# u, v and z as blocks with seven-product quads: a new order of the work, and x's place given to the branch inputs

## The chip, the cores and the metric

One core of a Trainium2 chip runs the whole kernel. The metric is the device time of one execution in microseconds (us). Matrix products run on TensorE (PE), elementwise work on VectorE (DVE) and ScalarE (ACT), a few small things on GpSimd (POOL); SyncE (SP) issues nearly all DMAs.

## The reference, cut to what matters

```
h = rms_norm(x, norm_g)                      # x: 256 x 4096 float32
proj = h @ w_in                              # 4096 x 22560
u, v, z_gm, qkv, z_dn, b, a, gate_gm, gate_dn = split_columns(proj)
y_gm = gmlp_spatial_gating(gelu(u), gelu(v), ln_g, ln_b, w_s, b_s)   # layer norm of v, 16 mixing matrices
y_gm = (y_gm * silu(z_gm)) @ w_br_gmlp       # 2048 x 4096
q, k, v = silu(causal_conv(qkv)) ...         # 16 heads of 128
o = rms_norm(gated_delta_rule(q, k, v, beta, g), dn_norm_g)
y_dn = (o * silu(z_dn)) @ w_br_dn            # 2048 x 4096
merged = sigmoid(gate_gm) * y_gm + sigmoid(gate_dn) * y_dn
out = rms_norm(x + merged @ w_out, final_g)  # 4096 x 4096
```

## The kernel before, in words

**Jobs.** `jobs` is a list of products with a weight matrix. A `Job` makes one chunk of 512 columns for both halves of the 256 rows: it walks over k in *pieces* of two k tiles of 128. Each float32 weight tile is loaded as `raw`, cast to a high part `wh` (ACT, L185) and a low part `wl` (DVE, L186); per k tile and row half three matmuls of 512 columns are issued (L196 to L198), so a piece has 12, a job over 4096 rows 192, a branch job (2048 rows) 96. x, as high and low part, lies in the eight `xs` tiles.

**Blocks.** A `Block` makes two neighbouring chunks together. For a pair of k tiles (a *quad*) the plain way needs 8 products of three matmuls; for the quads in `SEVEN` it needs 7, by a Strassen-Winograd scheme: pieces a, b, d, c (L225 to L230), with combinations of weights made on DVE (`tt`, L264 to L272) and combinations of x prepared once (`gforms`). Eight sums P1 to P8 fill all eight PSUM banks; `sums_out` (L987) adds them up into the two chunks. Only 12 of the 16 gate chunks are blocks here.

**Order.** Gates 0 and 2, six gate blocks, then for four groups of heads the jobs v, k, q, z of the delta part, then v0 to v3, gate 13, u0, z0, ... u3, z3, gate 15, 16 branch jobs (dn and gmlp of a chunk alternate), 8 jobs with `w_out`.

**Lanes.** Everything else is written as generators in two `lanes`: lane 0 takes what a finished job leaves (activations, convolutions, layer norm, mixing), lane 1 the delta rule of the groups (`dn_gen`, L765). `step` (L121) advances each lane to its next `yield`; `stream` (L282) calls it after every 12 matmuls. `drain` steps until a lane is empty. The order so written is a priority: the compiler's scheduler issues what is ready, so loads, ACT and DVE work may come earlier than written if nothing holds them.

**The delta part of a group.** `done_conv` scales a job's result, stores it, loads it back shifted three times and multiplies by `conv_w`; then `dn_gen` makes the 32x32 blocks (L776 to L816), inverts them by an elimination of 62 DVE operations (L825, L827), builds the 128x128 inverses by PE steps (L860 to L908), and makes o (L912 to L968), stored to `yds`. The branch inputs `ygs`, `yds` are loaded back as `yr` and cast to `ys` in `open_c` (L1027) during gate 15, into two `yr` buffers.

**Memory.** Pools are opened and closed in phases; a tile put where an older one was waits for that tile's last use. `px` (gate blocks), `pa` and `pq` (delta), `pv` and `pb` (gMLP), `pc` (branches), `pd` (output). `xs` is kept all along and takes the branch results at the end (L1078).

Of the kernel before, what the change touches and what calls it, by code (L numbers as in the profile page):

```python
# [9 lines left out]
F32 = mybir.dt.float32  # L10
# [23 lines left out]
SEVEN = (1, 3, 4, 6, 8, 9, 11, 13)  # L34

# [9 lines left out]
class Block:  # L45
# [3 lines left out]
    def __init__(self, w, col, nk, src, forms, done, before=None):  # L49
        self.w, self.col, self.nk, self.src, self.forms = w, col, nk, src, forms  # L50
        self.done, self.before = done, before
# [11 lines left out]
def trunk(ctx, tc, t):  # L63
# [4 lines left out]
    xtp = ctx.enter_context(tc.tile_pool(name="xtp", bufs=1))  # L68
# [49 lines left out]
    lanes = [[], []]  # L118
    wait = [0, 0]

    def step():  # L121
        for i, q in enumerate(lanes):
            if wait[i] > 0:
# [80 lines left out]
    def block_acc():  # L204

        nblk[0] += 1
        apart = ("P6", "P7") if nblk[0] % 2 == 0 else ("P3", "P8")
        return {n: bank() if n in apart else pm.tile([P, 512], F32, name="acc")
                for n in ("P8", "P4", "P2", "P3", "P1", "P6", "P5", "P7")}
# [51 lines left out]
    def quad_split(p, raw):  # L261
        r0, r1 = raw
        if p.kind == "a":
            t12 = px.tile([P, 2, NC], F32, name="tt", bufs=3)  # L264
            t34 = px.tile([P, 2, NC], F32, name="tt", bufs=3)
            V.tensor_tensor(out=t12[:, 0], in0=r0[:, 0], in1=r0[:, 1], op=ALU.add)
            V.tensor_tensor(out=t12[:, 1], in0=t12[:, 0], in1=r1[:, 0], op=ALU.subtract)
            h = px.tile([P, 1, NC], F32R, name="s2", bufs=7)
            l = px.tile([P, 1, NC], F32R, name="s2", bufs=7)
# [12 lines left out]
    def stream():  # L282
# [12 lines left out]
        state = dict(got=0, made=0, pairs=0, mm=0)  # L295

        def get(upto):
            while state["got"] < min(upto, len(order)):
# [3 lines left out]
                where = "wp" if room["wp"] else "x" if room["x"] and quad else None  # L302
# [8 lines left out]
                else:  # L311
                    raw = (wp if where == "wp" else px).tile([P, KPD, NC], F32, name="raw",
                                                             bufs=5 if where == "wp" else XRAW)
                    nc.sync.dma_start(out=raw, in_=j.w[k * P:(k + 1) * P, j.col:j.col + 2 * NC].rearrange(
                        "p (c n) -> p c n", c=2))
# [5 lines left out]
        def make():  # L321
            p = pieces[state["made"]]
            n = order.index(p.raws[-1])
            get(n + (4 if p.kind == "std" else 4 + XRAW))
# [13 lines left out]
        for c, p in enumerate(pieces):  # L338
# [4 lines left out]
            if p.first:  # L343
                if j.before:
                    j.before()
                acc = block_acc() if isinstance(j, Block) else [pm.tile([P, 512], F32, name="acc") for _ in range(2)]
            u = sp.pop(c)
            if isinstance(j, Block):
                quad_mms(p, *u, acc)
# [10 lines left out]
            state["mm"] += {"a": 3, "b": 6, "c": 6, "d": 6}.get(p.kind, 12)  # L360
            if state["mm"] >= 12:
                state["mm"] -= 12
                step()
# [6 lines left out]
    phx = ExitStack()  # L370
    px = phx.enter_context(tc.tile_pool(name="px", bufs=1))
    xraw = {}

    def first_x(i):
        if i < KT // KPD:
            xraw[i] = px.tile([P, KPD, S], F32, name="s2", bufs=7)
# [23 lines left out]
    def norm_gen():  # L400
        yield 12
        xend = xs[KT // 4 - 1][:, 1, 3, S - 1:S].bitcast(F32)
        for m in range(2):
            for c in range(8):
                xt = px.tile([P, NC], F32, name="s2", bufs=7)
# [32 lines left out]

    gforms = {q: px.tile([P, 2, 4, P], F32R, name=f"gf{q}") for q in SEVEN}

# [7 lines left out]
    def forms_gen():  # L448
        yield 15
        for q in SEVEN:  # L450
            x = xs[q // 2]
            k0 = 2 * q % 4
            a = px.tile([P, 2, 2, P], F32, name="s2", bufs=7)
            f = px.tile([P, 4, P], F32, name="s2", bufs=7)
# [16 lines left out]
    phb, phv = ExitStack(), ExitStack()  # L471
    pb = pv = None
    late_ = {}

    def open_v():
        nonlocal pv
        pv = phv.enter_context(tc.tile_pool(name="pv", bufs=1, side="right", reuse_waits="tile"))
        late_["vg"] = [pv.tile([P, W], F32, name=f"vg{m}") for m in range(2)]
        late_["vsum"] = pv.tile([P, 8], F32, name="vsum")

    def open_b():
        nonlocal pb
        pha.close()
        pb = phb.enter_context(tc.tile_pool(name="pb", bufs=1, reuse_waits="tile"))
        lng, lnb = (pb.tile([P, W], F32, name=n) for n in ("lng", "lnb"))
        wst, bs = pb.tile([P, 16, P], F32, name="wst"), pb.tile([P, 16], F32, name="bs")
        late_.update(lng=lng, lnb=lnb, wst=wst, bs=bs)
        nc.sync.dma_start(out=lng, in_=t["ln_g"].partition_broadcast(P))
        yield 2
        nc.sync.dma_start(out=lnb, in_=t["ln_b"].partition_broadcast(P))  # L490
        yield 2
        nc.sync.dma_start(out=wst, in_=t["w_sT"])
        nc.sync.dma_start(out=bs, in_=t["b_sT"])
        yield 2
        G.memset(wst[64:P, :, 0:64], 0.0)
        late_["open"] = True

    def need_b():
        while "open" not in late_:
            step()  # L500

    def done_v(c):
        def f(acc):
            if c == 0:
                drain((0,))
                phq.close()
                open_v()
            vg, vsum = late_["vg"], late_["vsum"]

            def gen():  # L510
                for m in range(2):
                    A.activation(vg[m][:, c * NC:(c + 1) * NC], acc[m], AF.Gelu,
                                 scale=rstd[:, m:m + 1], accum_out=vsum[:, m * 4 + c:m * 4 + c + 1])
                yield
                if c == 3:
                    yield from ln_gen()
            lanes[0].append(gen())
        return f

    def ln_gen():  # L520
        while "open" not in late_:
            yield
        vg, vsum, lng, lnb = (late_[n] for n in ("vg", "vsum", "lng", "lnb"))
# [17 lines left out]
        for c in range(4):  # L541
# [704 lines left out]
```

## Time and profile before

| | us |
|---|---|
| median of 3 runs (lowest, highest) | 2721.86 (2718.69, 2726.11) |
| the profiled execution | 2727.94 |
| its span, first to last instruction | 2725.8 |

The profile is of one execution. A row of stretches gives the busy time of each engine in a stretch of the span, the granted share of TensorE's clock and the DMA engines' share. Rows of groups give busy time, mean of one, and idle time ahead with what ended it. PE matmuls overlap in the trace (0.39 us each while a new one starts every 0.227 us), so their pace is read from a stretch and its count.

### The profile page before, as it was taken

The numbers are of one execution on the slowest core, as the hardware profiler recorded it, in microseconds if no ns is written. First come the engines' busy times: TensorE is split into PE (matmuls) and PEld (weight loads), VectorE is DVE, ScalarE is ACT, GpSimd is POOL, SyncE is SP. The second block draws the span as 40 slices with busy tenths as digits, with TensorE's granted clock in tenths as the row PEclk, the third lists the DMA queues.
The fourth block names the chain that finished last, engine by engine and source line by source line (L and its number), as shares of the span: only waits on it lengthen the run. The fifth ranks groups of instructions, "written<-read, shape, count | busy, mean of one in ns | idle before, by whom it ended". The sixth has DMA issues, their size and how long they took to land.

```text
span 2725.8 us, 33592 instructions
## 1 busy us (share of the span) xinstructions
PE 2688.8 (99%) x12241; PEld 2211.5 (81%) x12241; DVE 1843.5 (68%) x2475; ACT 1460.1 (54%) x2025; POOL 39.9 (1%) x40
## 2 busy tenths in 40 slices
PE   9999999999999999999999999999999999999998
PEld 7888888888878788778778888788888888888886
DVE  8898998975767857855875755655466666645544
ACT  7655555554554555545565544655465555644443
POOL 0000000000000000000000000000000000000000
PEclk9999999999999999999999999999999999999999
DMA  9766676777767858765965775676686666576665
GB/s 358 226 209 206 213 229 209 223 208 242 235 214 245 261 172 256 236 194 166 302 189 170 202 206 161 223 197 193 198 297 214 220 204 229 178 245 217 206 215 170
DMA packets 300718, 595.58 MB, mean 218 GB/s; under 512 B 33636, under 2 KB 47972, under 8 KB 300168
## 3 DMA queue, kind: packets, MB, share of 16 engines
q1 hardware_dynamic: 300264, 593.28, 70.0%
q8 instruction: 96, 1.57, 0.2%
q14 instruction: 70, 0.57, 0.1%
q10 hardware_dynamic: 288, 0.15, 0.0%
HBM read 569.16 MB, written 24.19 MB: 218 GB/s over the span
## 4 chain that ended last, share of the span: by engine, by line
PE 61%; issue 25%; DMA 6%; DVE 4%; ACT 2%; SPq 0%; POOL 0%; POOLq 0%; DVEq 0%; ACTq 0%
PE acc L197 20%; PE acc L196 20%; PE acc L198 20%; DVE wl L186 2%; DMA tok<-preq 1%; ACT wh L185 1%; DMA raw<-w_in 1%; DMA cw<-conv_w 1%; DMA preq<-tok 1%; ACT kT L154 1%; DVE tok L715 1%; DMA tok<-prek 0%; DVE tok L716 0%; PE side L579 0%; DMA tok<-prev 0%
## 5 line engine op out<-in xcount | busy, mean ns | idle before, releaser
L186 DVE TENSOR_TENSOR wl<-raw,wh 128x1024 fp32r<-128x1024 f32 x762 | 927.6, 1222 | 679.5 <-ACT wh L185 675.7
L185 ACT CAST wh<-raw 128x1024 fp32r<-128x1024 f32 x762 | 795.6, 1052 | 920.3 <-PE acc L198 832.4
L197 PE MATMUL acc<-wl,xs 128*128 128x512 f32 x2540 | 995.6, 392 | 14.0 <-DVE wl L186 13.5
L198 PE MATMUL acc<-wh,xs 128*128 128x512 f32 x2540 | 991.6, 391 | 0.0
L196 PE MATMUL acc<-wh,xs 128*128 128x512 f32 x2540 | 984.9, 392 | 4.9 <-ACT wh L185 4.1
L197 PEld LDWEIGHTS acc<-wl,xs 128*128 128x128 f32 x2540 | 478.5, 188 | 122.2 <-DVE wl L186 24.7
L196 PEld LDWEIGHTS acc<-wh,xs 128*128 128x128 f32 x2540 | 477.8, 188 | 107.4 <-ACT wh L185 6.7
L198 PEld LDWEIGHTS acc<-wh,xs 128*128 128x128 f32 x2540 | 478.5, 188 | 98.6
L258 ACT CAST wh<-raw 128x1024 fp32r<-128x1024 f32 x144 | 150.1, 1050 | 92.0 <-PE acc L239 51.9
L197 PE MATMUL acc<-wl,ys 128*128 128x512 f32 x512 | 199.2, 389 | 0.0
L198 PE MATMUL acc<-wh,ys 128*128 128x512 f32 x512 | 199.2, 389 | 0.0
L196 PE MATMUL acc<-wh,ys 128*128 128x512 f32 x512 | 195.8, 389 | 0.0
L259 DVE TENSOR_TENSOR wl<-raw,wh 128x1024 fp32r<-128x1024 f32 x144 | 174.0, 1222 | 10.2 <-ACT wh L258 9.9
L238 PE MATMUL acc<-wl,xs 128*128 128x512 f32 x384 | 150.3, 391 | 0.0
L239 PE MATMUL acc<-wh,xs 128*128 128x512 f32 x384 | 149.9, 390 | 0.0
L237 PE MATMUL acc<-wh,xs 128*128 128x512 f32 x384 | 125.0, 391 | 0.0
L258 ACT CAST wh<-tt 128x1024 fp32r<-128x1024 f32 x96 | 100.2, 1049 | 39.4 <-PE acc L239 25.5
L259 DVE TENSOR_TENSOR wl<-tt,wh 128x1024 fp32r<-128x1024 f32 x96 | 116.0, 1222 | 4.4 <-ACT wh L258 4.2
L198 PEld LDWEIGHTS acc<-wh,ys 128*128 128x128 f32 x512 | 96.1, 188 | 20.1
L197 PEld LDWEIGHTS acc<-wl,ys 128*128 128x128 f32 x512 | 96.1, 188 | 20.0
L196 PEld LDWEIGHTS acc<-wh,ys 128*128 128x128 f32 x512 | 96.1, 188 | 19.8
L238 PEld LDWEIGHTS acc<-wl,xs 128*128 128x128 f32 x384 | 72.1, 188 | 16.1
(273 smaller groups left out, 2151.7 us busy)
## 6 DMA issues: line engine op xcount, KB each, us to landing
raw<-w_in SPq DMA_DIRECT2D x703, 512.0 KB
raw<-w_out SPq DMA_DIRECT2D x128, 512.0 KB
raw<-w_br_dn SPq DMA_DIRECT2D x64, 512.0 KB
raw<-w_br_gmlp SPq DMA_DIRECT2D x64, 512.0 KB
cw<-conv_w SPq DMA_DIRECT2D x48, 256.0 KB
sgs<-sg SPq DMA_DIRECT2D x16, 512.0 KB
sg<-sgs SPq DMA_DIRECT2D x16, 512.0 KB
tok<-prev SPq DMA_DIRECT2D x12, 512.0 KB
```

Of the source, the lines that this page charges most:

```text
L154: A.copy(o, i)
L185: A.copy(h, raw)
L186: V.tensor_tensor(out=l, in0=raw, in1=h.bitcast(F32), op=ALU.subtract)
L196: T.matmul(acc[m], lhsT=xh, rhs=h[:, kk], start=f, stop=False)
L197: T.matmul(acc[m], lhsT=xh, rhs=l[:, kk], start=False, stop=False)
L198: T.matmul(acc[m], lhsT=xl, rhs=h[:, kk], start=False, stop=e)
L237: T.matmul(acc[name], lhsT=xh, rhs=h[:, i], start=f, stop=False)
L238: T.matmul(acc[name], lhsT=xh, rhs=l[:, i], start=False, stop=False)
L239: T.matmul(acc[name], lhsT=xl, rhs=h[:, i], start=False, stop=e)
L258: A.copy(h, src)
L259: V.tensor_tensor(out=l, in0=src, in1=h.bitcast(F32), op=ALU.subtract)
L715: V.tensor_tensor(out=h[:, m], in0=h[:, m], in1=cw, op=ALU.mult)
```

## The change

- Gates 13 and 15 become a seventh gate block. v becomes two blocks, and u and z of a chunk one block each (their columns lie 4096 apart, so a block now has two start columns and loads two pieces of a row). These six use seven products in the five quads of `SEVEN_B`, with buffers of pool `psv`: two `tt`, and no extra `raw` tiles beyond the five.
- P1, P6, P5, P7 get their PSUM banks only at a block's first seven-product quad; mixing takes a `spare` bank.
- Order: gates, v, u/z, delta groups, the eight gmlp branch jobs, the eight dn branch jobs, `w_out`. The products of the gmlp half go back to `sgs` and are loaded again in the dn half.
- After the last delta job `open_c` drains lane 0, closes `pq` and x's pool, and puts `ys` there; inputs 0 to 3 are loaded and cast at once through one `yr` buffer, 4 to 6 in a new lane 2 as the groups end, 7 at the end of group 3. The branch results go to new tiles `xo`.
- Where lane 0 is empty, lane 1 gets a second step per 12 matmuls. `ln_g` and `ln_b` come in four parts each.

```diff
+SEVEN_B = (4, 6, 8, 11, 13)
...
+    def spare():
+        return bank() if nblk[0] % 2 == 0 else pm.tile([P, 512], F32, name="acc")
...
-            t12 = px.tile([P, 2, NC], F32, name="tt", bufs=3)
-            t34 = px.tile([P, 2, NC], F32, name="tt", bufs=3)
+            pool, n = p.job.ext
+            t12 = pool.tile([P, 2, NC], F32, name="tt", bufs=n)
+            t34 = pool.tile([P, 2, NC], F32, name="tt", bufs=n)
...
+            if state["mm"] >= 6 and not state["half"]:
+                state["half"] = True
+                if not lanes[0]:
+                    step((1,))
...
+    def done_uz(c):
+        def f(acc, p):
+            job = p.job
+            if p.first:
+                job.u = pb.tile([P, 2, NC], F32, name="gu", bufs=2)
+                job.z = pb.tile([P, 2, NC], F32, name="zt", bufs=2)
+                job.out = sums_out(acc, p, lambda i, m: (job.z if i else job.u)[:, m])
...
     def open_c():
-        done_by()
-        phv.close()
-        phb.close()
-        pc = phc.enter_context(tc.tile_pool(name="pc", bufs=1, reuse_waits="tile"))
+        drain((0,))
+        phq.close()
+        phx.close()
+        pc = phc.enter_context(tc.tile_pool(name="pc", bufs=1, side="right", reuse_waits="tile"))
+        for i in range(8):
+            ys[i] = pc.tile([P, 2, 4, S], F32R, name=f"ys{i}")
         def gen():
+            for i in range(4, 7):
+                while dn_done[0] < i - 3:
+                    yield
+                yield from get_y(i)
+        for i in range(4):
+            for _ in get_y(i):
+                pass
+        lanes[2].append(gen())
+
+    def get_y(i):
+        yr = pc.tile([P, 4, S], F32, name="yr", bufs=1)
+        nc.sync.dma_start(out=yr, in_=(ygs + yds)[i])
+        yield 3
+        A.copy(ys[i][:, 0], yr)
+        V.tensor_tensor(out=ys[i][:, 1], in0=yr, in1=ys[i][:, 0].bitcast(F32), op=ALU.subtract)
+        yield 3
+
+    def open_y():
+        pha.close()
+        py = phy.enter_context(tc.tile_pool(name="py", bufs=1, reuse_waits="tile"))
+        for d in range(8):
+            xo[d] = py.tile([P, 2, 4, S], F32R, name=f"xo{d}")
+        for _ in get_y(7):
+            pass
...
+    def before_br(d, second):
         def f():
+            while second and (not xo or lanes[2]):
                 step()
...
-    for i in (1, 4, 5, 8, 9, 12):
+    for i in (1, 4, 5, 8, 9, 12, 13):
+        c0 = gcol[i % 2] + i // 2 * NC
+        jobs.append(Block(win, (c0, c0 + NC), KT, xsrc, gforms, (px, 3), done_gates(i), need_forms))
+    for c in (0, 2):
+        c0 = V0 + c * NC
+        jobs.append(Block(win, (c0, c0 + NC), KT, xsrc, bforms, (psv, 2), done_v(c), None if c else open_b))
+    for c in range(4):
+        jobs.append(Block(win, (U0 + c * NC, ZG0 + c * NC), KT, xsrc, bforms, (psv, 2), done_uz(c)))
...
+    for second in range(2):
+        for d in range(8):
+            jobs.append(Job(t["w_br_dn"] if second else t["w_br_gmlp"], d * NC, KT // 2,
+                            (lambda k, s=second * 4: (ys[s + k // 4], k % 4)), done_br(d, second),
+                            before_br(d, second)))
+
+    def last_x(acc, f=jobs[first + 15].done):
+        f(acc)
+        open_c()
+    jobs[first + 15].done = last_x
```

## Rows read from the trace of the kernel before

**Rows 1.** The page's first part: busy us, share of the span, instructions
```profile
PE 2688.8 (99%) x12241; PEld 2211.5 (81%) x12241; DVE 1843.5 (68%) x2475; ACT 1460.1 (54%) x2025; POOL 39.9 (1%) x40
```
**Rows 2.** Stretches: us; busy us of the engines with counts; clock, DMA share, GB/s
```profile
core 0: us, PE busy (x) PEld busy (x) DVE busy (x) ACT busy (x) POOL busy (x), PEclk, DMA share, GB/s
96.00:593.00 497.00, 497.00 (x2162) 405.47 (x2161) 448.92 (x520) 290.54 (x315) 0.00 (x0) 1.00 0.69 213
...
2018.20:2366.30 348.10, 348.10 (x1537) 288.27 (x1536) 209.73 (x258) 192.24 (x313) 0.00 (x0) 1.00 0.67 219
592.95:1359.23 766.28, 751.90 (x3525) 616.66 (x3524) 529.35 (x806) 400.51 (x569) 22.16 (x14) 1.00 0.75 230
1359.23:1408.57 49.34, 46.27 (x193) 36.82 (x192) 44.24 (x93) 30.64 (x58) 3.73 (x2) 0.97 0.69 201
1408.57:1460.12 51.55, 51.55 (x314) 42.27 (x312) 26.45 (x42) 28.47 (x47) 0.96 (x1) 1.00 0.62 175
1555.60:1599.12 43.52, 43.52 (x193) 36.04 (x192) 28.52 (x57) 19.50 (x22) 0.95 (x1) 1.00 0.72 200
1697.66:1752.05 54.39, 48.56 (x213) 39.98 (x212) 39.67 (x74) 38.27 (x84) 1.65 (x2) 0.94 0.67 216
```
**Rows 3.** Groups of instructions of DVE, then ACT, 96 to 593 us
```profile
L259 DVE TENSOR_TENSOR wl<-raw,wh 128x1024 fp32r<-128x1024 f32 x143 | 172.8, 1222 | 10.2 <-ACT wh L258 9.9
...
L267 DVE TENSOR_TENSOR tt<-tt,raw 128x512 f32<-128x512 f32 x47 | 32.4, 690 | 5.8 <-DMA raw<-w_in 5.6
...
L258 ACT CAST s<-raw 128x512 fp32r<-128x512 f32 x46 | 28.6, 621 | 64.8 <-DMA raw<-w_in 64.8
```
**Rows 4.** Waits of PE, 1359 to 1760 us: total, times, longest
```profile
PE side L579 <- DVE vg L546: 5.8, 1, 5.8
```
**Rows 5.** Stretches at the pause in u1
```profile
1723.00:1728.80 5.80, 0.01 (x1) 0.00 (x0) 5.80 (x10) 2.26 (x3) 0.00 (x0) 0.83 0.34 124
1728.80:1733.00 4.20, 4.16 (x14) 3.71 (x15) 4.20 (x6) 0.00 (x0) 0.00 (x0) 0.50 0.43 126
```
**Rows 6.** Timeline of DVE: first and last elimination operation, groups 2 and 3
```profile
1360.65 0.42 DVE L825 TENSOR_TENSOR tm<-xs,big 128x248 f32<-128x248 f32 x1
...
1411.62 0.18 DVE L827 TENSOR_TENSOR xs<-xs,tm 128x8 f32<-128x8 f32 x1
...
1537.45 0.42 DVE L825 TENSOR_TENSOR tm<-xs,big 128x248 f32<-128x248 f32 x1 [1.10 <-DMA big<-nscr]
...
1574.56 0.18 DVE L827 TENSOR_TENSOR xs<-xs,tm 128x8 f32<-128x8 f32 x1
```
**Rows 7.** Timeline of SP and PE: stores of groups 2 and 3, L860 of 3
```profile
1493.35 4.17 SPq L968 DMA_DIRECT2D yds<-vtok  x2
...
1631.86 1.09 PE L860 MATMUL side<-tmp,nt 32*32 32x32 f32 x32
...
1702.69 0.54 SPq L968 DMA_DIRECT2D yds<-vtok  x1
```
**Rows 8.** Timeline of ACT: first scale, last copies of q0 and q3
```profile
732.40 0.69 ACT L700 ACTIVATE tok<-acc,rstd 128x512 f32<-128x512 f32 x1 [0.59 <-PE acc L198]
...
775.87 1.23 ACT L154 COPY qT<-tmp 32x128 f32<-32x128 f32 x4
...
1325.48 1.27 ACT L700 ACTIVATE tok<-acc,rstd 128x512 f32<-128x512 f32 x2 [4.71 <-DVE ktok L716]
...
1379.93 3.69 ACT L154 COPY qT<-tmp 32x128 f32<-32x128 f32 x12
```
**Rows 9.** Timeline of SP, ACT, DVE: one branch input is loaded and cast
```profile
1993.17 0.34 SPq L1037 DMA_DIRECT2D yr<-yds  x1
...
1999.27 1.05 ACT L1040 CAST ys<-yr 128x1024 fp32r<-128x1024 f32 x1 [1.58 <-DMA yr<-yds]
...
2000.35 2.59 DVE L1041 TENSOR_TENSOR ys<-yr,ys 128x1024 fp32r<-128x1024 f32 x2 [1.40 <-ACT ys L1040]
```

More of the change, by code (lines that the diff above doesn't have):

```diff
@@ L116, in rs, with step @@
         G.tensor_tensor(out=out, in0=in_, in1=half[:, 0:n], op=ALU.pow)
-    lanes = [[], []]
-    wait = [0, 0]
-    def step():
+    lanes = [[], [], []]
+    wait = [0, 0, 0]
+    def step(only=(0, 1, 2)):
         for i, q in enumerate(lanes):
+            if i not in only:
+                continue
             if wait[i] > 0:
@@ L301, in get @@
                 quad = isinstance(j, Block)
-                where = "wp" if room["wp"] else "x" if room["x"] and quad else None
+                more = quad and j.ext[0] is px
+                where = "wp" if room["wp"] else "x" if room["x"] and more else None
                 if where is None:
@@ L345, in stream @@
                     j.before()
-                acc = block_acc() if isinstance(j, Block) else [pm.tile([P, 512], F32, name="acc") for _ in range(2)]
+                acc = {} if isinstance(j, Block) else [pm.tile([P, 512], F32, name="acc") for _ in range(2)]
+                if isinstance(j, Block):
+                    nblk[0] += 1
+                    block_acc(acc, ("P8", "P4", "P2", "P3"))
             u = sp.pop(c)
             if isinstance(j, Block):
+                if p.kind == "a" and "P1" not in acc:
+                    block_acc(acc, ("P1", "P6", "P5", "P7"))
                 quad_mms(p, *u, acc)
@@ L436, in const_gen @@
             yield
-    gforms = {q: px.tile([P, 2, 4, P], F32R, name=f"gf{q}") for q in SEVEN}
+    gforms = {q: (psv if q in SEVEN_B else px).tile([P, 2, 4, P], F32R, name=f"gf{q}") for q in SEVEN}
+    bforms = {q: gforms[q] for q in SEVEN_B}
     def sums(dst, a):
@@ L470, in trunk @@
     lanes[1].append(const_gen())
[L471 to L479, printed above, removed]
+    phb = ExitStack()
+    pb = None
+    gm = {}
     def open_b():
         nonlocal pb
-        pha.close()
+        done_by()
+        phw.close()
@@ L489, in open_b @@
[L489 to L517, printed above, removed]
+        gm.update(wst=wst, bs=bs)
@@ new lines, in gen, with done_v, z @@
+        def gen():
+            yield 4
+            nc.sync.dma_start(out=wst, in_=t["w_sT"])
+            nc.sync.dma_start(out=bs, in_=t["b_sT"])
+            yield 2
+            G.memset(wst[64:P, :, 0:64], 0.0)
+        lanes[1].append(gen())
+    def done_v(c0):
+        def f(acc, p):
+            vg, vsum = gm["vg"], gm["vsum"]
+            def z(c, m):
+                return vg[m][:, (c0 + c) * NC:(c0 + c + 1) * NC]
+            if p.first:
+                p.job.out = sums_out(acc, p, z)
+            if next(p.job.out, "end") == "end":
+                def gen():
+                    for c in range(2):
+                        for m in range(2):
+                            A.activation(z(c, m), z(c, m), AF.Gelu, scale=rstd[:, m:m + 1],
+                                         accum_out=vsum[:, m * 4 + c0 + c:m * 4 + c0 + c + 1])
+                        yield
+                    if c0 == 2:
+                        yield from ln_gen()
+                lanes[0].append(gen())
@@ L1047, in trunk, with sg @@
     sig, part = {}, {}
-    def before_br(i):
+    def sg():
+        return pc.tile([P, 2, NC], F32, name="sg", bufs=4)
+    def before_br(d, second):
         def f():
-            while i == 0 and "all" not in ys:
+            while second and (not xo or lanes[2]):
                 step()
-            sig[i] = pc.tile([P, 2, NC], F32, name="sg", bufs=4)
-            nc.sync.dma_start(out=sig[i], in_=sgs[i])
-        return f
-    def done_br(i):
-        d, second = i // 2, i % 2
+            sig[d] = sg()
+            nc.sync.dma_start(out=sig[d], in_=sgs[2 * d + second])
+            if second:
+                part[d] = sg()
+                nc.sync.dma_start(out=part[d], in_=sgs[2 * d])
+        return f
@@ L1065, in gen @@
                     V.tensor_tensor(out=s[:, m], in0=acc[m], in1=s[:, m], op=ALU.mult)
-                if second:
-                    part[d] = s
+                if not second:
                     yield
+                    nc.sync.dma_start(out=sgs[2 * d], in_=s)
                     return
```

165 lines of the change are left out of this document (68 added, 97 removed).

## The prediction
> **What bounds the kernel now.** I read the busy times of the engines first: the reader sees TensorE (PE) busy for 2688.8 of 2725.8 us and VectorE (DVE) for 1843.5 [rows 1]. So only two things can move the time: fewer matmuls, or fewer and shorter pauses of PE. Then the stretches by stage [rows 2], each from the first matmul of a job to that of the next. A plain job (192 matmuls; gate 13, 1555.60 to 1599.12) takes 43.52 us, and all the branch jobs together 348.10 us for 1536 matmuls: 0.2267 us a matmul, no pause. The six blocks take 497.00 us for 6 x 360 matmuls, 82.83 us each, with DVE busy for 448.92 us, and PE still without a pause; the ACT casts of the seventh-operand pieces wait 64.8 us in all for weights, none of which reaches PE [rows 3]. The delta stage (592.95 to 1359.23) is 766.28 us for 16 plain jobs, 696.3 us of work: 70 us are its small matmuls and pauses. Third, two jobs that are too long: v0 (49.34 us, no small matmuls in it) and u1 (54.39 us) [rows 2]. The view of PE's waits names the second: small matmul L579 waits 5.8 us for the layer norm's last operation [rows 4]. Last, the timeline of the delta chain [rows 6, 7] and of the conversion of the branch inputs [rows 9], because the change moves both.
>
> **The sevens.** A block of two column chunks replaces two plain jobs, 87.04 us. With eight quads of seven products it takes 82.83 us, so a quad of seven costs (82.83 - 8 x 24 x 0.2267)/8 = 4.91 us against 5.44 us, a gain of 0.526 us. That is less than its three matmuls (0.68 us): the others of such a quad start about 0.234 us apart. The change adds one gate block (8 quads) in place of two jobs and six blocks of five quads: 38 x 0.526 = **20.0 us** less. The upper bound is 38 x 3 x 0.2267 = 25.8 us; the lower bound is nothing, if something else binds these blocks.
>
> A rule that would price it higher: the Trainium skill, page "TensorE: Matmul & The Clock Gate", section "Part 1: The HAM clock gate", gives N/2.4 GHz plus about 2.5 ns for a matmul at full clock, 215.7 ns at 512 columns. The trace does not agree: 226.7 ns in plain jobs and 234 ns in quads of seven [rows 2]. By the page, 114 matmuls would be worth 24.6 us (an estimate); the sum keeps 20.0 us.
>
> Does DVE bind the new blocks? A plain quad costs DVE two operations of 1.222 us, one of seven three of these and five of 0.69 us [rows 3]: 7.1 against 2.4 us. Three quads of seven fewer take 14 us from the 74.8 us that a gate block keeps DVE busy (448.92/6), which leaves 61 us; the lane work adds 15 us in the block with the layer norm (some 24 operations of about 0.6 us) and 7 in the others (u*z, mixing, transposes), estimates from the same rows; the nine readings-out of sums are in the 74.8 already. 68 to 76 of 84.4 us: looser than what already runs without a pause. What is tighter is buffers: two `tt` instead of three, five raw weight tiles instead of eight. Plain jobs live on five raws. I cost it at **+3 us** over all six blocks (0 to +16; at +16 the sevens there give nothing), start-up with four `s2` buffers included. The DMAs of `w_sT`, `ln_g` and `ln_b` enter SP's queue among the raws, where four pieces of lead (10.9 us) cover them. Gelu and Silu now read SBUF in place of PSUM, as many operations as before.
>
> **Pauses that go.** v0 and u1 lose what made them long. v0 is 5.8 us too long, with the drain of the last q convolution before it. u1 is 54.39 - 43.52 - 2.6 (20 small matmuls) = 8.3 us too long: the late opening of the pool pushes the layer norm directly ahead of L579, and after the 5.8 us pause the granted clock is 0.50 (1.2 of 2.4 GHz) over the next 4.2 us [rows 5]. In the new order the norm has 28 steps of the 31 in block u0/z0, and its first columns are ready long before block u1/z1. **-14.1 us** (0 to -14.1).
>
> **The handover after the last delta job.** Now `ys` takes the place of x, and nothing but `ys` can feed PE after zd3. `open_c` drains lane 0: conv q3 is emitted in full there. It waits for nothing of PE's and may run earlier: its scale needs only the q3 job, which ends 43.5 us (some 47 with small matmuls) before zd3 does. From first scale to last transposed copy q0 took 45 us (732.4 to 777.1) and q3 58 us (1325.5 to 1383.6) [rows 8]. So it ends between -2 and +11 us from the end of zd3. Its token tiles lie where pool `pc` now lies, so `ys` or `yr` starts after it. Then `yr` has one buffer and the four loads follow one another: load 6.1 us (1993.17 to 1999.27), cast 1.05, subtraction 1.2 [rows 9], 8.4 us each, while PE eats one `ys` in 24 x 0.2267 = 5.44 us. If the first is ready at +6, the fourth is ready at 6 + 25 = +31 and wanted at +16: PE loses about 15 us, and a slow clock after each pause some more, 2 us by half of the 4.2 us at 0.50 in [rows 5]. I take **+16 us**. Bounds: +2 (loads hoisted into zd3, only the chain left) and +34 (conv late, all four loads behind it).
>
> **The delta chain's end.** One lane step goes with 12 matmuls (2.72 us). Counting the yields, the change's second step of lane 1 whenever lane 0 is empty puts the last step of group 3 at 732 matmuls (166 us) after zd3, and the gmlp half of the branches ends at 768 (174 us): no burst of empty steps. But the chain has its own pace. Its elimination took 51 us in group 2 (1360.65 to 1411.8) and 37 in group 3 (1537.45 to 1574.7) [rows 6], and from there to the store of the result 82 to 86 us in group 2; in group 3, 71 us from L860 on [rows 7], which leaves some 12 for the steps before it. With group 2's elimination beginning 38 us before zd3's end, it ends at +13, group 2 at +98. Its tile `big`, one buffer, is free some 15 us earlier, so group 3's elimination runs from +89 to +126 and its store is at +211; load and cast of `ys7` 8 us: **+219**. The dn half begins at 174 + 16 (handover) + about 20 (small matmuls of one and a half groups; v1, full of them, is 8.0 us over) = +210 and wants `ys7` in its seventh piece, 16 us later: +226. Just in time: 0, bounds 0 and +30.
>
> **The rest of the branches.** Products of the first half go to `sgs` and back: 8.4 MB more over 348 us where 219 GB/s at 0.67 of the DMA engines flow [rows 2]; hidden. Each dn job of 21.8 us has a whole chunk to turn (16 small copies and two transposes on ACT and DVE): about 17 us of each engine with the casts; tight, hidden by the lead. The w_out stage is the same.
>
> **The sum** is made against the profiled execution's 2727.94 us (span 2725.8 and 2.1 around it): 2727.9 - 20.0 - 14.1 + 16 + 3 = 2712.8. That execution is 6.1 us above the median of the runs, 2721.86, so on the runs' scale: 2706.7, **2707 us**; its own range is 2697 to 2713.
>
> **Rivals.** (1) *Handover free*: conv q3 done inside zd3, loads hoisted. For it: q0's 45 us; against it: `yr` has one buffer. 14 to 16 us less: 2692. (2) *The new blocks bind elsewhere* (raws late with five buffers): for it, the 64.8 us of ACT waits on weights with eight [rows 3]; against it, PE paused nowhere. 16 us more: 2723. (3) *Handover at its upper bound*: +34 for +16: 2725. (4) *The other side*: the delta chain ends late, and the dn half cannot start. PE stands still for it because no other work is left that doesn't need `ys7`; it decides from a store of group 3 later than about +218 us after zd3. If group 2 and group 3 don't overlap (the `big` tile and `tmp2` hold group 3 back to +98 for its first step; first phase 40, elimination 37, rest 85) `ys7` comes at +268: 42 us late, 2749. For it: group 3's store came 209 us after group 2's (1493.35 to 1702.69); against it: there 57 us lie between its elimination and L860, whose turn had not come [rows 6, 7]. That the change does not issue fewer matmuls is no rival: the products are counted in its pieces.
>
> **Chances.** Forecast 0.44; (1) 0.18; (2) 0.09; (3) 0.12; (4) 0.17, of which some 0.07 between 2730 and 2736. The measurement of this kernel tells 0.3% (8.2 us) from no change: faster is below 2713.7, slower above 2730.0. Faster 0.44 + 0.18 = 0.62; same 0.09 + 0.12 = 0.21; slower 0.17. The range reaches from rival (1) with the upper bound of the sevens to the weak end of (4): 2688 to 2736.
>
> **What would show it.** Blocks of v and u/z at 84.4 us and the seventh gate block at 82.8; u/z blocks without a wait of L579. After zd3 a wait of PE on the cast or subtraction of `ys`, the four `ys` some 8 us apart, and a slice of half clock. In the first dn job at most a short wait on `ys7`. It is wrong if the blocks take 87 us, if PE stands at `ys7` for over 10 us, or if the delta jobs themselves, which I left at 766 us, change.

## The result, and the profile after

The changed kernel takes 2770.11 us (median of 4 runs, 2769.01 to 2770.36) beside 2722.46 us for the kernel before (median of 4): a ratio of 1.0174, 95% interval 1.0157 to 1.0192. It is slower by 47.7 us where 2707 us, faster, was forecast. The profiled execution took 2769.92 us, with a span of 2768.1.

The first part of the page of the changed kernel, to be read beside [rows 1]:

```profile
PE 2717.8 (98%) x12127; PEld 2197.9 (79%) x12127; DVE 2029.5 (73%) x2759; ACT 1518.6 (55%) x2104; POOL 38.3 (1%) x40
```

PE has 114 instructions fewer, the 38 quads' three each, and is busy 29 us *longer*. So the loss isn't only pauses. The stretches say where it lies (us; busy time and count of each engine; clock, DMA share, GB/s). They are, in order: the second plain job, the seven gate blocks, v with u and z, the delta jobs, the handover (from the last matmul of zd3, the z job of the last head group, to the first branch matmul), the branches, and one block and one branch job alone:

```profile
53.83:98.81 44.98, 44.98 (x194) 36.21 (x192) 34.37 (x62) 33.83 (x61) 3.83 (x11) 1.00 0.83 279
98.81:685.92 587.11, 587.11 (x2522) 474.28 (x2520) 527.22 (x609) 339.11 (x368) 0.00 (x0) 1.00 0.69 211
685.92:1210.50 524.58, 522.72 (x2264) 422.20 (x2263) 414.54 (x510) 302.05 (x385) 2.42 (x2) 1.00 0.65 203
1210.50:1989.40 778.90, 770.33 (x3541) 619.04 (x3539) 550.59 (x873) 423.27 (x634) 23.45 (x16) 1.00 0.74 227
1989.40:2016.07 26.67, 4.19 (x66) 3.58 (x65) 16.00 (x51) 9.06 (x22) 0.95 (x1) 0.56 0.46 152
2016.07:2408.54 392.47, 389.61 (x1813) 315.44 (x1813) 263.94 (x404) 223.17 (x394) 5.10 (x3) 0.99 0.68 222
...
685.92:772.02 86.10, 86.10 (x371) 69.49 (x369) 64.34 (x72) 45.41 (x48) 0.95 (x1) 1.00 0.67 219
2122.59:2145.09 22.50, 22.50 (x98) 18.11 (x97) 21.06 (x46) 8.43 (x8) 0.00 (x0) 1.00 0.77 256
```

**A plain job takes 44.98 us without one pause,** at a granted clock of 1.00, where 43.52 was read before [rows 2]: 234.3 ns a matmul instead of 226.7. The quiet branch job (22.50 for 21.76) and the block (86.10 for 369 matmuls, 233.3 ns) are slow in the same way, with PE busy throughout. The w_out jobs, which read a new tensor `xo`, stayed at 43.52.

**The handover costs 26.7 us.** PE's waits from 1980 to 2050 us (total, times, longest), and SP's:

```profile
PE side L869 <- DVE tmp L861: 18.9, 3, 18.4
PE side L881 <- ACT tmp L873: 3.0, 1, 3.0
```
```profile
SPq L847 <- DVE xs L836: 6.0, 1, 6.0
SPq L1056 <- DMA yr<-ygs: 5.3, 2, 3.9
```

Not a branch matmul waits here but L869, the first product of a delta group's chain, which stands ahead of all branch jobs in PE's order. The timelines of DVE, SP and PE show what it stands behind (start, duration, engine, line, operation):

```profile
2002.59 0.17 DVE L836 TENSOR_TENSOR xs<-xs,tm 128x8 f32<-128x8 f32 x1
2007.42 0.30 DVE L861 STREAM_TRANSPOSE tmp<-big 32x128 f32<-32x128 f32 x1 [4.66 <-DMA big<-xscr]
...
2009.39 0.66 DVE L149 STREAM_TRANSPOSE tmp<-tok 128x512 f32<-128x512 f32 x1
```
```profile
2002.79 1.72 SPq L847 DMA_DIRECT2D xscr<-xs  x4
2005.71 3.64 SPq L851 DMA_DIRECT2D big<-xscr  x8
...
2009.92 0.38 SPq L1056 DMA_DIRECT2D yr<-ygs  x1
2017.60 6.93 SPq L1056 DMA_DIRECT2D yr<-ygs  x2
2029.94 0.34 SPq L1056 DMA_DIRECT2D yr<-ygs  x1
```
```profile
1989.03 0.40 PE L202 MATMUL acc<-wh,xs 128*128 128x512 f32 x1
2007.87 0.60 PE L869 MATMUL side<-tmp,nt 32*32 32x32 f32 x8 [18.44 <-DVE tmp L861]
...
2016.07 0.80 PE L200 MATMUL acc<-wh,ys 128*128 128x512 f32 x1
```

Group 2's elimination ends at 2002.8, its result goes out to memory and back, and only then can PE go on; the first `yr` load stands in SP's queue behind the same result. `open_c` drains lane 0 by advancing *all* lanes, so 26 steps of the chain are written in one burst with no branch matmul between them. From 1993 on, through the rest of the pause and behind it, the clock is low:

```profile
1993.00:2023.00 30.00, 11.10 (x91) 8.97 (x92) 14.41 (x50) 8.77 (x23) 0.95 (x1) 0.50 0.48 164
```

Last, the first job of the dn half (27.42 us for 22.49) waits for the last `ys`. It is seen as a wait for `wh`: ACT's cast of weights stands behind the cast of `ys7`, which waits for its load (PE's waits, 2223 to 2255; then SP and ACT).

```profile
PE acc L200 <- ACT wh L189: 2.1, 1, 2.1
```
```profile
2237.10 4.22 SPq L977 DMA_DIRECT2D yds<-vtok  x2
2243.42 0.34 SPq L1056 DMA_DIRECT2D yr<-yds  x1
```
```profile
2247.13 1.05 ACT L1058 CAST ys<-yr 128x1024 fp32r<-128x1024 f32 x1 [3.38 <-DMA yr<-yds]
```

The stages in us, with the forecast's terms laid on the same scale: 99 is 96 and the 3 of the buffers, 522 is the 659 of these jobs before less gates 13 and 15 (87), the pauses (14.1), the sevens (15.8) and the 20 of small matmuls that move to the branches. The last two columns are kernels of the next two sections; the kernel before has its jobs in another order and no column.

| stage | forecast | after | e1_align | e9_1250 |
|---|---|---|---|---|
| to the first block | 99 | 98.8 | 103.8 | 104.9 |
| seven gate blocks | 579.8 | 587.1 | 579.0 | 578.8 |
| v, u, z | 522 | 524.6 | 512.4 | 514.0 |
| delta, to zd3's last matmul | 766.3 | 778.9 | 765.2 | 758.2 |
| handover | 16 | 26.7 | 27.3 | 21.5 |
| branches | 368 | 392.5 | 388.2 | 376.5 |
| w_out and end | 359.5 | 359.6 | 359.5 | 359.5 |

### The profile page after: what moved, and what is told of

Same layout as the page of the kernel before. It is cut to its first block, busy times and chain, and to the rows that moved or that the text cites. A ratio compares the mean times of both kernels' runs of the same rounds, so it can differ in the third digit from the quotient of the medians.

```text
span 2768.1 us, 33861 instructions
## 1 busy us (share of the span) xinstructions
PE 2717.8 (98%) x12127; PEld 2197.9 (79%) x12127; DVE 2029.5 (73%) x2759; ACT 1518.6 (55%) x2104; POOL 38.3 (1%) x40
## 4 chain that ended last, share of the span: by engine, by line
PE 87%; DMA 4%; DVE 4%; issue 2%; ACT 2%; POOL 0%; SPq 0%; DVEq 0%; POOLq 0%; ACTq 0%
PE acc L200 15%; PE acc L201 15%; PE acc L202 15%; PE acc L245 10%; PE acc L246 10%; PE acc L244 10%; PE side L245 3%; PE side L244 3%; PE side L246 3%; DVE wl L190 1%; DMA raw<-w_in 1%; DMA cw<-conv_w 1%; ACT wh L189 1%; DMA preq<-tok 1%; DMA prek<-ktok 0%
## 5 line engine op out<-in xcount | busy, mean ns | idle before, releaser
L190 DVE TENSOR_TENSOR wl<-raw,wh 128x1024 fp32r<-128x1024 f32 x538 | 654.4, 1222 | 403.2 <-ACT wh L189 401.3
L189 ACT CAST wh<-raw 128x1024 fp32r<-128x1024 f32 x538 | 560.7, 1050 | 620.6 <-PE acc L202 547.9
L265 ACT CAST wh<-raw 128x1024 fp32r<-128x1024 f32 x330 | 344.4, 1050 | 234.0 <-PE acc L246 118.3
L201 PE MATMUL acc<-wl,xs 128*128 128x512 f32 x1152 | 458.4, 399 | 7.2 <-DVE wl L190 7.0
L200 PE MATMUL acc<-wh,xs 128*128 128x512 f32 x1152 | 455.3, 399 | 3.6 <-ACT xs L415 2.1
L202 PE MATMUL acc<-wh,xs 128*128 128x512 f32 x1152 | 452.6, 397 | 0.0
L266 DVE TENSOR_TENSOR wl<-raw,wh 128x1024 fp32r<-128x1024 f32 x330 | 398.3, 1220 | 54.9 <-ACT wh L265 54.7
L246 PE MATMUL acc<-wh,xs 128*128 128x512 f32 x888 | 352.0, 396 | 0.0
L245 PE MATMUL acc<-wl,xs 128*128 128x512 f32 x888 | 352.0, 396 | 0.0
L244 PE MATMUL acc<-wh,xs 128*128 128x512 f32 x888 | 299.4, 396 | 0.0
L201 PEld LDWEIGHTS acc<-wl,xs 128*128 128x128 f32 x1152 | 217.2, 189 | 63.7 <-DVE wl L190 13.4
L200 PEld LDWEIGHTS acc<-wh,xs 128*128 128x128 f32 x1152 | 217.0, 189 | 57.6 <-ACT xs L415 3.7
L202 PEld LDWEIGHTS acc<-wh,xs 128*128 128x128 f32 x1152 | 217.2, 189 | 51.4
L265 ACT CAST wh<-tt 128x1024 fp32r<-128x1024 f32 x172 | 179.3, 1050 | 100.4 <-PE acc L246 54.4
L266 DVE TENSOR_TENSOR wl<-tt,wh 128x1024 fp32r<-128x1024 f32 x172 | 208.3, 1222 | 18.6 <-ACT wh L265 17.6
L202 PE MATMUL acc<-wh,ys 128*128 128x512 f32 x512 | 205.3, 402 | 0.0
L200 PE MATMUL acc<-wh,ys 128*128 128x512 f32 x512 | 201.6, 402 | 2.2 <-ACT wh L189 2.1
L246 PEld LDWEIGHTS acc<-wh,xs 128*128 128x128 f32 x888 | 167.4, 189 | 40.3
L245 PEld LDWEIGHTS acc<-wl,xs 128*128 128x128 f32 x888 | 167.2, 188 | 40.4
L244 PEld LDWEIGHTS acc<-wh,xs 128*128 128x128 f32 x888 | 167.0, 188 | 39.6
L201 PE MATMUL acc<-wl,xo 128*128 128x512 f32 x492 | 191.6, 389 | 0.0
```

What stands on the lines that cost most here:

```text
L189: A.copy(h, raw)
L190: V.tensor_tensor(out=l, in0=raw, in1=h.bitcast(F32), op=ALU.subtract)
L200: T.matmul(acc[m], lhsT=xh, rhs=h[:, kk], start=f, stop=False)
L201: T.matmul(acc[m], lhsT=xh, rhs=l[:, kk], start=False, stop=False)
L202: T.matmul(acc[m], lhsT=xl, rhs=h[:, kk], start=False, stop=e)
L244: T.matmul(acc[name], lhsT=xh, rhs=h[:, i], start=f, stop=False)
```

## The experiments: the pace

Why does the same matmul take 234 ns? A line of the change that the diff above leaves out put x's pool at the right end of the partition, and `pc`, with ys, is there too:

```diff
-    xtp = ctx.enter_context(tc.tile_pool(name="xtp", bufs=1))
+    phx = ExitStack()
+    xtp = phx.enter_context(tc.tile_pool(name="xtp", bufs=1, side="right"))
```

In these products 128 columns of xs or ys are the stationary operand and 512 columns of `wh` or `wl` the moving one. By the program's own allocation xs, ys, `wh` and `wl` all stood at 128 mod 256 bytes before; after it xs and ys stand at 224, `wh` and `wl` still at 128, and `xo`, whose jobs stayed fast, at 128. Theory A: the place of one operand against the other sets the pace. Rivals: the far end of the partition, or other work on the memory.

**e1_align**: the changed kernel, 96 bytes of padding behind xs and ys.
```
+    xtp.tile([P, 24], F32, name="padx")
+        pc.tile([P, 24], F32, name="padc")
```


> The changed kernel with 96 bytes of padding in x's pool and in the pool of ys, which moves xs and ys from an SBUF address 32 bytes past a multiple of 64 to one on it; both stay at the top of the partition. Theory A (a stationary tile off 64 bytes makes every matmul start 0.2343 us after the last in place of 0.2267): 18 plain jobs x 1.46 + 16 branch jobs x 0.73 + 7 blocks x 1.06 + 6 x 1.7 = 55.6 us less, 2714 us, and the 27 us pause after zd3 stays. Rival B (the top of the partition, far from the weight tiles, is slow to read): 2770, no change. Rival C (DVE and ACT, busier in the new order, get in PE's way): 2770, no change.

Measured: 2736.77 us, ratio to before 1.0056 (1.0039 to 1.0072), 33 us less than the changed kernel, where theory A counted 55.6. Plain jobs are back at 43.52, and a block of v runs at 226.7 ns:

```profile
766.40:850.04 83.64, 83.64 (x371) 69.26 (x370) 64.00 (x71) 45.47 (x53) 0.00 (x0) 1.00 0.64 202
```

That is 369 x 0.22667 to the digit: a quad of seven saves its three whole matmuls, 0.68 us. Part of the rest goes into waits that the faster pace uncovers: the second plain job now takes 51.6 us, because SP's queue holds the weights behind loads of x into too few `tt` tiles (50 to 106 us):

```profile
SPq L430 <- ACT tt L432: 14.9, 12, 3.7
SPq L430 <- POOL tt L116: 8.2, 1, 8.2
```

**e2_xs32**: the kernel before, xs moved by 32 bytes and all tiles behind it by 128, so that xs stands at 160 and `wh` and `wl` at 0 mod 256, while ys and the weight halves stay level. **e5_both32**: xs and all tiles behind it, the weight halves among them, moved by 32.
```
+    xtp.tile([P, 8], F32, name="padx")     (e2 and e5, ahead of xs)
     xs = [xtp.tile([P, 2, 4, S], F32R, name=f"xs{k}") for k in range(KT // 4)]
+    xtp.tile([P, 24], F32, name="pady")    (e2 alone: the tiles behind xs keep their place mod 128)
```


> The kernel before with 32 bytes of padding ahead of xs and 96 behind, so that xs alone is 32 bytes off 64, at its old low place; the work is the same. Theory A: 40 plain jobs x 1.46 = 58 us and 6 blocks x 1.1 to 1.5 more, 2787 us; branch jobs stay at 21.76 us each. Rivals B and C: 2722, no change.

> The kernel before with 32 bytes of padding ahead of xs only: xs and the weight tiles wh, wl (the moving operand) are both 32 bytes off 64. If only their difference counts: 2722. If one of them off is as bad as both: all 11376 big matmuls at 0.2343, 2808. If each adds its own: 0.241, 2885.

Measured: e2 2762.93 us, ratio 1.0151, by an edit of nothing but places. Theory A had 2787: it took the pace of a difference of 96 bytes, and this is one of 160. e5 2719.83 us in a single run, as before. So it is the difference of the two places that counts, not a place itself; the end of the partition and other work on the memory are refuted as causes, since neither changed in e2 and e1_align stays at that end.

**e3_xs64**: xs moved by 64 bytes and the tiles behind it by 128, to 192 and 0 mod 256. **e6_px0**: the quads' forms and sums moved by 64, from 192 to 0 mod 256. **e7_px192**: the same tiles moved by 192, to 128 mod 256, where xs and `wh` are.
```
+    xtp.tile([P, 16], F32, name="padx")    (e3, ahead of xs and again behind)
+    px.tile([P, 16], F32, name="padx")     (e6; 8 more ahead of the last pieces)
+    px.tile([P, 48], F32, name="padx")     (e7; 40 more ahead of the last pieces)
```


> The kernel before with xs moved by 64 bytes (xs at 64, the weight halves at 0 mod 128 bytes). Theory (the matmul's pace hangs on the difference of the two operands' places mod 128 bytes, as quads of seven at 64 mod 128 went at about 234 ns): plain jobs and w_out-free stages go at .2333 to .2343 instead of .2267, plain jobs 44.8 instead of 43.5, the whole about 2755 to 2765. Rival (only the difference mod 64 counts): nothing changes, 2722 within 0.3 per cent.

> The kernel before with 64 bytes of padding ahead of the working tiles of the quads (forms and sums then at 0 mod 128 like xs and the weight halves) and 32 bytes ahead of the last pieces' tiles. Theory (alignment): the quads of seven in the six gate blocks go from 234 to 227 ns a matmul, blocks 82.8 to about 81.6, out7 44.1 to 43.5; the whole about 2714 (2710 to 2718), faster than before by 0.3 per cent. Rival (the 234 ns of these quads come from their sums on the vector engine or from their own shapes, not from the place): no change, 2722.

> The kernel before with 192 bytes of padding ahead of the quads' working tiles and 160 ahead of the last pieces' tiles, so that their place equals that of xs and the weight halves mod 256 bytes, not only mod 128. Theory (the pace hangs on the difference of the two operands' places mod 256 bytes; a difference of 64 took .2336, of 96 .2343, of 128 .2328, of 160 .2333, of 192 .2289 us a matmul, of 0 .2267): gate blocks go from 82.8 to 81.6, out7 from 44.1 to 43.5, the whole to 2712 to 2718, faster than before by some 0.3 per cent. Rival (the quads of seven are slower by their own shape, and only mod 128 counts): no change, 2722.

Measured: e3 2735.51 (1.0034 to 1.0061), slower, but by less than the 2755 to 2765 of its theory; e6 2722.87 (0.9990 to 1.0007); e7 2718.00 (0.9971 to 0.9989). One row of each: gate 13 in e2, e3 and e5, a gate block in e6 and e7 (beside 82.8 us in [rows 2]).

```profile
1571.20:1616.00 44.80, 44.80 (x193) 36.04 (x192) 28.47 (x56) 19.43 (x22) 0.96 (x1) 1.00 0.70 193
```
```profile
1557.78:1601.72 43.94, 43.94 (x193) 36.06 (x192) 28.49 (x56) 19.45 (x22) 0.95 (x1) 1.00 0.72 198
```
```profile
1547.60:1591.12 43.52, 43.52 (x193) 36.04 (x192) 28.47 (x57) 19.50 (x22) 0.95 (x1) 1.00 0.71 198
```
```profile
177.53:260.48 82.95, 82.95 (x361) 67.64 (x360) 76.26 (x91) 49.64 (x55) 0.00 (x0) 1.00 0.70 218
```
```profile
95.86:177.46 81.60, 81.60 (x362) 67.59 (x360) 73.33 (x84) 47.24 (x51) 0.00 (x0) 1.00 0.71 219
```

e6 was a miss that told more than a hit: equal places mod 128 are not enough. e7 has them equal mod 256, and its blocks run at 226.7 ns where they don't wait (360 x 0.22667 = 81.60). The 234 ns of the sevens in [rows 2] had nothing to do with quads of seven; their forms stood 64 bytes off. Of some 7 us that e7 sought it kept 5.4, the rest went into waits of two blocks (83.65 and 82.77 us).

## The experiments: the handover

**e4_drain0**: the changed kernel (not aligned), the burst taken away.
```
-            step()
+            step(only or (0, 1, 2))
```


> The changed kernel where the drain of lane 0 steps lane 0 alone, so that the delta steps of lane 1 are not written ahead of the loads of ys. Theory D (after zd3 the first branch input waits in SP's queue and DVE's behind the delta chain): the pause of 27 us and its 3 us of slow clock shrink to about 10, 15 to 20 us less there; the delta chain is written 26 steps later and may cost 5 to 15 at the dn half: 2755 to 2765. Rival E (conv q3 and the single yr buffer alone set it): 2770 within 3.

Measured: 2777.14 us, ratio 1.0202 (1.0187 to 1.0217): no gain, 7 us more than the changed kernel, where 5 to 15 less were expected. From zd3's last matmul to the first of the branches 10.6 us pass instead of 26.7, but the chain is then late at the end (PE's waits, 2225 to 2280 us):

```profile
PE acc L200 <- ACT ys L1058: 16.1, 1, 16.1
```

So the burst only moves the price. The chain itself is late, and the next question is by what.

**e8_cut** (e1_align, the elimination cut to its first column) and **e9_1250** (e1_align, where the elimination gives up its turn at 1250 ns of estimated work, not at 700; the kernel before had 700 while lane 0 had work and 1250 otherwise).
```
-        for j in range(SUB - 1):
+        for j in range(1):                 (e8)
-            if done > 700:
+            if done > 1250:                (e9)
```


> The changed kernel aligned (as e1_align), with the elimination of each delta group cut to its first column: 60 of its 62 vector operations and the 30-odd turns that they take are left out. Theory (what stays over in the aligned kernel is the delta chain that ends too late: at the handover and again at the last ys): both waits go, the gap behind zd3 and the stretch at half clock with it, 2737 goes to about 2695 to 2705, below the kernel before. Rival (the handover is late because the first yr load waits for memory that the delta stage holds, or because its casts queue in the vector engine): zd3 to brG0 still takes over 85 us, the whole stays above 2720.

> The changed kernel aligned (as e1_align), with one edit of the change taken back in part: the elimination gives up its turn every 1250 ns of estimated work instead of every 700, some 7 turns fewer in a group. Theory (the chain is late by its turns, 2.72 us each): the chain of the last group ends about 19 us earlier, the handover's loss shrinks by 10 to 20 us: 2717 to 2727. Rival (each turn carries more vector work, which then holds up the weight halves' casts and PE, as the vector engine is busy about 0.9 in that stage): delta jobs grow by as much as the handover gives, 2733 to 2742.

Measured: e8 2710.23 us (ratio 0.9933 to 0.9964). e9 2712.01 us, ratio 0.9963 (0.9949 to 0.9977), **25 us less than e1 by an edit of one number, and 0.37% below the kernel before**; its theory had 2717 to 2727. The eliminations of groups 1 and 2, first and last operation of each, in e1 and then in e9:

```profile
1671.87 0.42 DVE L835 TENSOR_TENSOR tm<-xs,big 128x248 f32<-128x248 f32 x1 [5.98 <-DMA big<-nscr]
...
1757.38 0.18 DVE L837 TENSOR_TENSOR xs<-xs,tm 128x8 f32<-128x8 f32 x1
...
1918.98 0.42 DVE L835 TENSOR_TENSOR tm<-xs,big 128x248 f32<-128x248 f32 x1 [0.82 <-DMA big<-nscr]
...
1974.19 0.17 DVE L837 TENSOR_TENSOR xs<-xs,tm 128x8 f32<-128x8 f32 x1
```
```profile
1662.00 0.42 DVE L835 TENSOR_TENSOR tm<-xs,big 128x248 f32<-128x248 f32 x1 [2.59 <-DMA big<-nscr]
...
1722.07 0.17 DVE L837 TENSOR_TENSOR xs<-xs,tm 128x8 f32<-128x8 f32 x1
...
1880.50 0.42 DVE L835 TENSOR_TENSOR tm<-xs,big 128x248 f32<-128x248 f32 x1 [0.92 <-issue]
...
1954.25 0.17 DVE L837 TENSOR_TENSOR xs<-xs,tm 128x8 f32<-128x8 f32 x1
```

Group 2's elimination ends 20 us earlier, 15 us earlier against zd3's end. But the theory's reason does not give it: the loop has 13 turns at 700 and 8 at 1250, so 5 fewer, 13.6 us at 2.72 each, not 7 (and e8 leaves out 13, not some 30). And the gain is not spread so. Group 1's elimination took 60 us in place of 86, group 2's could begin 38 us earlier and then took longer, 74 in place of 55; group 0's did not change. So that fewer turns bring the gain is shown, and how they do is not. Group 3 gains too, and the wait for the last `ys` is gone (branches 388.2 to 376.5 us). The delta jobs did not grow, they went from 765.2 to 758.2: the rival is refuted (in the changed kernel DVE was busy for 0.71 of that stage, not about 0.9). e8, which leaves out nearly the whole elimination, took away the wait for the last `ys` too, but came out above its theory's 2695 to 2705. It says that the elimination's own operations are not the rest: with hardly any of them 18.6 us still pass at the handover, behind an operation of the last group's first step (PE's wait for L786, 11.1 us) and behind `ys` (4.5 us).

**e10_both** (e9 and e4's edit) and **e11_all** (e10 with the gate blocks' tiles at 128 mod 256).

> As e9_1250 (aligned, turns of 1250 ns), and only lane 0 advanced while its jobs' ends are drained at the handover, so that the last group's steps are not written in a burst with no matmuls between them. Theory (two separate prices at the handover: the burst, some 15 us, and the chain's lateness, which the fewer turns took away): zd3 to brG0 loses 12 to 18 us less, and the last ys comes in time or up to 10 us late: 2694 to 2706. Rival (the steps not done in the burst make the chain late again, as in e4_drain0, where brD1 waited 19 us): 2710 to 2722.

> As e10_both, and the gate blocks' own working tiles padded by 192 bytes, so that all quads of seven stand at difference 0 mod 256 bytes. Theory (mod 256): gate blocks lose some 0.4 us each (82.05 to 81.6), 3 us in all below e10_both, the best of the kernels. Rival: no difference to e10_both beyond 0.1 per cent.

Measured: 2716.17 (0.9965 to 0.9986) and 2714.13 us (0.9952 to 0.9977). Without the burst the handover takes 12.0 instead of 21.5 us, but the branches take 385.7 instead of 376.5: the first two jobs of the dn half (brD0, brD1) wait again, 4.2 us for `wh` the longest. The rival was right, as in e4. e11 lies 2 us below e10, where 3 were expected. The intervals of e9, e10 and e11 overlap; which is best is open.

**e12_yrq** (e9), **e13_yrq0** (e10): `yr` loaded by POOL's queue. **e14_best**: e12 with e11's padding.
```
-        nc.sync.dma_start(out=yr, in_=(ygs + yds)[i])
+        nc.gpsimd.dma_start(out=yr, in_=(ygs + yds)[i])
```


> As e9_1250 (aligned, turns of 1250 ns), with the loads of the branch inputs (yr) issued by POOL instead of SP, where the first stands behind the store of the elimination's result and, once out, behind the reads of it. Theory (the rest of the handover's price is the yr loads' place in SP's order): the first load goes out when the last matmul of zd3 has freed the memory, up to 16 us sooner, and the gap behind zd3 (16 us in e9_1250) halves or better: 2700 to 2708. Rival (PE waits there for the chain's own vector work, put ahead of the branch jobs in PE's order by the burst): no change, 2710 to 2714.

> As e10_both (aligned, 1250, no burst) with the yr loads issued by POOL. In e10_both PE waited 11.8 us for the first cast of yr, whose load went out at 1962.6 behind the xscr store at 1960.8, while zd3's matmuls were through about 1953. Theory (SP's order): that wait shrinks to 5 to 7 us (a load of 3.7 us and a cast), and the delta chain's tail then waits more at brD0 or brD1 (4.2 us in e10_both, up to 12): net 2708 to 2714. Rival (the memory under yr comes free no sooner): no change, 2716.

> As e12_yrq with the gate blocks' working tiles padded by 192 bytes (difference 0 mod 256 bytes for all quads of seven). Theory: 2 to 3 us below e12_yrq, the fastest kernel of all, 2698 to 2706. Rival: the gate blocks give the pace back to waits for weight halves, as e7_px192 did in part, and there is no difference to e12_yrq.

Measured: 2718.63 (0.9976 to 0.9993), 2723.40 (0.9988 to 1.0006), 2716.40 us (0.9967 to 0.9985). e12 and e13 are above e9 and e10, and none reaches its theory's range; e14 is 2 us below e12, as its theory had it, but the intervals overlap. In e12 the load does go out early, and its cast comes 19 us after the landing at 1960.1, behind the chain's copies in ACT's order (POOL, then ACT); the handover grew from 21.5 to 26.2 us:

```profile
1953.59 0.76 POOL L1058 DMA_DIRECT2D yr<-ygs  x1
```
```profile
1978.18 0.65 ACT L918 ACTIVATE big<-side 64x256 f32<-64x256 f32 x2 [2.06 <-PE side L915]
1978.85 1.04 ACT L1060 CAST ys<-yr 128x1024 fp32r<-128x1024 f32 x1
```

In e13, without the burst, POOL's queue holds the load behind a memset that waits for the elimination as SP's store did (POOL's waits):

```profile
POOL big L845 <- DVE tm L835: 12.4, 1, 12.4
```

So e13 never freed the load, and did not test what it was meant to. In e13 the load stands behind a part of the chain, in e12 its cast does.

**e15_cut0**: e8 with e4's edit.

> As e8_cut (aligned; the elimination of each group cut to its first column, so 60 of 62 vector operations a group are left out), and without the burst: only lane 0 is advanced while its ends are drained. Theory (at the handover two things cost, each by itself: the delta group's steps written in a burst, behind which PE, ACT and SP stand in order, and the load and cast of the first ys, 5 to 8 us): in e8_cut 25 us are over from zd3 to brG0, of these the burst's 15 to 18 go, and the tail has slack enough not to wait: 2692 to 2700. Rival (the loss is the memory of yr, or the last q convolution, and comes whichever way the steps are written): zd3 to brG0 still loses over 20 us, 2706 to 2712.

Measured: 2698.01 us (0.9902 to 0.9935), within the theory's range, but by luck, not by its reason. The handover fell only from 18.6 to 13.4 us, not by 15 to 18; the other 8 us lie ahead of the delta jobs, which began at 1192.2 instead of 1200.2 by shorter waits that the edit does not touch. What is left of the handover is one wait of 11.1 us, for an operation of the last group that DVE does behind the copies of the last q convolution:

```profile
PE side L790 <- DVE tmp L786: 11.1, 1, 11.1
```

So no single cause of the last 10 to 20 us was found: the burst, q3's copies and the chain stand in for one another. That part stays open.

## Why the prediction was wrong, step by step

- **The pace: the step that failed first.** The prediction says that "only two things can move the time: fewer matmuls, or fewer and shorter pauses of PE", and prices a matmul at 226.7 ns outside the quads of seven. There is a third thing, the distance of matmuls that don't pause. The move of `xtp` to the right side got no term, and it cost 33 us (after against e1_align), more than the sevens were to bring. The sign was at hand: the prediction read 0.234 us in the quads of seven and used it as a price without asking for its cause, which e7 shows to be the place.
- **The sevens**, -20.0: the mechanism held and the size was too small. Aligned, a quad of seven saves 0.68 us (e1's v blocks, 83.64 = 87.04 - 5 x 0.68), the upper bound; in the changed kernel the slow pace swallowed it: 86.1 us for the v blocks and some 87.9 for those of u and z (of which their mixing products take some 2), forecast at 84.4, and 83.9 for the seventh gate block, forecast at 82.8. "Wrong if the blocks take 87 us" came true for u and z, though not for want of buffers.
- **Block buffers**, +3: 98.8 us to the first block for the forecast 99 is luck, since the slow pace of two plain jobs makes the 2.8. In e1_align, without it, the buffers cost 8 us in the second plain job: of x loads, which the step named only as "start-up".
- **Pauses that go**, -14.1: right. v has no pause, and the mixing products (L587, L579 before) never wait; PE waits 1.8 us in u/z0, for casts.
- **The handover**, +16: the failed step where the runs show more. Its total stayed inside the bounds of +2 to +34, but not its mechanism. It asked when conv q3, the convolution of the last q job, ends and how fast four `yr` loads follow. The loads came 5.7 to 7.7 us apart, near the 8.4 taken. Conv q3's last transposition came 20 us after zd3, beyond the bound of 11, because it too stood behind the chain, in DVE's order (L149 at 2009.39). The step put group 2's elimination at "+13" after zd3 (it ended at +13.4) and gave that no price at the handover, because it counted PE's order as branch jobs with chain between them. The burst puts the chain's products ahead of them: 26.7 us, and 30 us at clock 0.50; of these 30, the 7 us with branch matmuls lost about 3.5 at half pace, an estimate. Where the burst is gone, PE's longest wait at the handover is for `ys`, as the step had it: 10.4 us in e4, 11.8 in e10.
- **The delta chain's end**, 0: `ys7` was forecast at +219 and wanted at +226; it was ready at +260 and wanted at +251, since both slid. The first dn job took 4.9 us too long, inside the bounds (0 to +30); 2.9 of these are pauses. Rival (4) had the place right and the size too large: its wait is seen best where the burst is gone, 16.1 us in e4, of its 42.
- **Delta jobs left at 766 us**: they took 778.9. The pace alone adds 16 x 1.46 = 23; PE's idle time there fell from 14.4 to 8.6 us, and the rest of the difference was not followed. The elimination's turn, at 700 ns always and no longer at 1250 where lane 0 is empty, has no price in the prediction. Group 1's elimination took 84 us for 64 before; taking the turn to 1250 ends group 2's 20 us earlier and brings 25 us of the whole (e1 against e9).
- **The rest of the branches**, 0: 392.5 for 368, of which 11.7 is pace and 4.9 the first dn job; the other 8 were not measured apart.

Pace (33) and turns (25) together are 58 of the 63 us by which the forecast missed. With both mended the change is worth -0.37% (e9), close to the 2707 that the prediction reached without either. That nearness is luck in part: in e9 the jobs of v, u and z and the delta jobs take 16 us less than forecast, and start, handover and branches 20 us more. The low end of the range, 2688, is 2686 by its own terms (2692 less 5.8); nothing hangs on it.

## To carry to other kernels

When a change moves a tensor that PE reads, compare the two operands' byte places mod 256 before anything else. In this kernel a slow matmul without a pause, at full clock, was the sign, and a few bytes of padding the cure. And before pricing a drain or a barrier by what it waits for, list everything that it writes into the engines' orders on the way: here steps of another lane issued there stood ahead of the work that followed, on PE, DVE, ACT and SP alike. How often a chain gives up its turn can be worth as much as a faster matmul: one number moved the whole by 25 us here.

## What the runs showed of the hardware

The spacing of matmuls (128x512, f32 as a high and a low part, clock 1.00) against the stationary operand's place less the moving one's, mod 256 bytes. The columns at 64 and 128 are means over 366 neighbouring products with forms in the quads of seven, which alternate with others; the rest are from whole plain jobs:

| difference | 0 | 64 | 96 | 128 | 160 | 192 |
|---|---|---|---|---|---|---|
| ns a matmul | 226.7 | 233.1 | 234.3 | 233.4 | 233.3 | 228.9 |
| seen in | before, e1, e5, e7 | before | after | e6 | e2 | e3 |

In e7 the forms lie an odd multiple of 256 bytes from `wh`, by the allocation, and still run at 226.7: so 256 is period enough. Other differences were not tried, and why it is so no run shows. The Trainium skill, page "SBUF — State Buffer", section "SBUF: two separate sides", says that PE never waits on another engine there, and its part "A bandwidth-pool intuition that's wrong (but worth ruling out)" gives the weight load a second, independent read port; no run here contradicts the first, and the trace does not agree with the second as far as the pace goes: it hung on the places of both reads together, 44.80 us for 43.52 in e2_xs32 at a difference of 160 bytes.

Second, in the changed kernel the granted clock was 0.50 (1.2 of 2.4 GHz) from 1993 to 2023 us. PE had stopped at 1989.4; it worked again from 2007.9 on, in small products with pauses, and from 2016.1 on in branch matmuls 0.43 us apart.
